# Row sums of a hybrid layer's FFN as one task that requests ahead, and a compression bank that isn't cleared

## The chip, the cores and the metric

The kernel runs on one core of one Trainium2 chip. The metric is the device time of one execution in microseconds (us). The core's engines run their own queues of instructions and wait for each other through semaphores: TensorE (PE in the profile: matrix products), VectorE (DVE), ScalarE (ACT), GpSimd (POOL) and SyncE (SP, which only issues DMAs here; POOL issues some too).

## The reference

One decoder layer for 256 tokens of width 2048, in float32. One input projection feeds two groups of heads, gated linear attention (GLA) and a sparse attention (NSA); an output projection joins them, and a SwiGLU feed-forward network (FFN) follows. The part of NSA that the change touches is the compression of keys and values: 15 overlapping blocks of 32 tokens for each of 2 heads get a position vector added and go through a small network.

```python
def hybrid_layer(...):
    n = rms_norm(x, attn_norm_g)
    proj = n @ w_in
    ...
    h = x + jnp.concatenate([gla_out, nsa_out], axis=-1) @ w_out
    m = rms_norm(h, ffn_norm_g)
    return h + (jax.nn.silu(m @ w_gate) * (m @ w_up)) @ w_down

def compress(u, pos, w1, w2):
    blocks = u[:, :, cmp_idx] + pos
    flat = blocks.reshape(b_, hk, n_cmp, CMP_BLOCK * dh)
    return jax.nn.silu(flat @ w1) @ w2
```

## The kernel before

**Products.** Each float32 product is made of three matmuls: an operand is split into a high part (`hi`, rounded by ACT, L144) and a low part (`lo`, what is left, by DVE, L145), and `chunk` (L292) issues hi x hi, hi x lo and lo x hi. Weights of the two projections come in blocks of 1 MB (`raw`, three buffers) through SP's queue; a block is asked for when the third block before it has been split. These products run from the start of the kernel almost without a break to about 420 us; the FFN fills the rest.

**The FFN's row sums.** Most of the FFN runs as a scheme that needs 7 products of sub-blocks in place of 8 (L1164), at the price of sums of rows of the weights. Sixteen of these sums (a column block f and a pair of row blocks: (0,4), (1,2) to (1,5), (2,7) to (9,7), (10,2), (10,5), (10,7)) are made long ahead, beside the projections and mixers: `sum_rows` asks for two tiles of rows through SP (0.5 MB each, `gate` and `up`, L1091), makes four additions on DVE in place (L1096) and stores the two results to DRAM through POOL's queue (L1100). The FFN fetches them from there (L1153).

**What sets the order.** The order on each engine is that of the program. `drive` takes the projections' matmuls one group of three at a time, 2 units each. Whenever a count of units reaches `rate[0]`, the first task of `background` goes one step; and for each `pace` units a step of `urgent` or `later` goes (the mixers' small work). So `rate` says how many units lie between two steps of a sum: 12, then 26, 18, 14 and 14 in the five stages. A sum takes nine steps: the request, two empty ones, four additions, the store, one empty.

**The mixers' places.** Scores are normalised with a power of -0.5 on POOL (`rsqrt_`, L220): DVE L631 in front and L633 behind it in GLA's output, where L637 and L638 then scale (L655 makes a low part); L731, L732 in front and L734, L737 behind it for NSA's keys, which PE then transposes (L217).

**Compression.** `w1_rows` (L771) asks through POOL's queue for a half of a layer's weights, as two tiles; `positions` (L780) adds the position vectors on DVE, two instructions; then 16 matmuls (L796) add up into four groups of 30 rows of a PSUM bank, at a distance of 32. The bank is cleared first by DVE (L788) as the groups' last two rows are never written but are read with the rest (L803). Two such groups of 16 belong to the key, two to the value. A group's matmul j needs tile j // 8 of the weights.

**Buffers.** Rows of the sums, weights of the compression and other tiles of 4 KB per partition share one pool of 24 (`g4`): each takes the place of an older tile, and waits for all that read it.

Of the kernel before, what the change touches and what calls it, by code (L numbers as in the profile page):

```python
# [8 lines left out]
F32 = mybir.dt.float32  # L9
# [3 lines left out]
ALU = mybir.AluOpType  # L13
AX = mybir.AxisListType

P = 128
# [10 lines left out]
NCMP = 15  # L27
# [10 lines left out]
def kernel(  # L38
# [736 lines left out]
    def positions(w, half, new):  # L775

        blk, j0 = new([16, 2, NCMP]), 16 * half
        for h in range(2):
            u = st["uT"][:, w, h, j0:j0 + 240].rearrange("p (n j) -> p j n", j=16)
            TT(blk[:, :, h, :], u, pos[:, w, j0:j0 + 16].unsqueeze(2).to_broadcast([P, 16, NCMP]), ALU.add)  # L780
        return blk

    def compress():

        nxt = [st["rows"], w1_rows(1)]
        for w in range(2):
            ph = bank()
            nc.vector.memset(ph[:, :P], 0.0)  # L788
            for half in range(2):
# [4 lines left out]
                for j in range(16):  # L794
                    g = 32 * (j % 4)
                    mm(ph[g:g + N2, :P], blk[:, j].rearrange("p h n -> p (h n)"), r[j // 8][:, j % 8, :], start=(half == 0 and j < 4),  # L796
                       stop=(half == 1 and j >= 12), tile_position=(0, g), skip_group_check=True)
                    if j % 16 == 15:
                        yield
# [285 lines left out]
    def sum_rows(f, pair):  # L1085

        n_tiles[0] += 1
        gate, up = g4([2, 512]), g4([2, 512])
        for to, m in ((gate, w_gate), (up, w_up)):
            with behind(last["dma"]):  # L1090
                nc.sync.dma_start(to, m[0][2 * pair * P:(2 * pair + 2) * P, f * FB:(f + 1) * FB].rearrange("(k p) w -> p k w", p=P))  # L1091
        for _ in range(3):
            yield True
        for o, i in ((up[:, 0], up[:, 1]), (up[:, 1], gate[:, 1]), (gate[:, 1], up[:, 0]), (gate[:, 0], gate[:, 1])):
            with behind(last["d"]):
                TT(o, o, i, ALU.add)  # L1096
            yield True
        to = row_sums[f, pair] = [dp.tile([P, 2, 512], F32, name=f"sums{i}_{f}_{pair}") for i in range(2)]
        for part, a in zip(to, (up, gate)):
            nc.gpsimd.dma_start(part, a)  # L1100
        for _ in range(1):
            yield True
# [265 lines left out]
    background += [sum_rows(f, pair) for f in sorted(SUMS) for pair in SUMS[f]]  # L1368
    rate[0] = 12
# [3 lines left out]
    rate[0] = 26  # L1373
# [3 lines left out]
    rate[0] = 18  # L1377
    drive([proj(C_NQ + 512, ev_nq(1))], 2.5)
    rate[0] = 14
# [3 lines left out]
    rate[0] = 14  # L1383
# [43 lines left out]
```

## Time and profile before

| | |
|---|---|
| median of 3 executions | 1103.51 us (1102.64 to 1104.92) |
| profiled execution | 1103.67 us |
| its span | 1102.0 us |
| FFN's matmuls, L1164 and L292 on `ftwo` | 431.7 us and 221.1 us busy |
| DVE L1096, 64 additions | 0.69 us each |
| DMA from 50 to 100 us | 350 GB/s |

The span is what the trace covers; the rest of the execution's time lies around it. A timeline row reads: start, duration, engine, line, operation, output and inputs, partitions x elements; in brackets, how long the engine sat idle before it and for which engine's result. PE is TensorE's matmuls. Waits are also listed by group: engine and line that waited, what it waited for, the sum in us, how often, the longest. A chain's shares tell whose work the end of the kernel hangs on.

### The profile page before, as it was taken

The page shows a single profiled execution, that of the slowest core. Times are in us where ns is not written, and L with a number is a line of the kernel's source. Part 1 is how long each engine was busy: PE and PEld are TensorE (multiplying, and loading weights), DVE is VectorE, ACT ScalarE, POOL GpSimd, SP SyncE. Part 2 cuts the span into 40 slices and gives each one's busy share as a digit, 9 for nine tenths or more (in the row PEclk, how much of TensorE's full clock was granted, in tenths as well). Part 3 has the DMA queues.
Part 4 walks back from the last instruction along what each step waited for, and adds up shares of the span by engine and source line. Part 5 has one row for each costly group of instructions (what it writes and reads, how often), then busy time and mean ns, then how long its engine had stood idle before and what let it go on. Part 6 is the DMA issues. An engine that isn't in the chain of part 4 may idle for free.

```text
span 1102.0 us, 14594 instructions
## 1 busy us (share of the span) xinstructions
PE 1094.4 (99%) x5290; PEld 900.6 (82%) x5290; DVE 991.5 (90%) x1277; ACT 742.0 (67%) x1009; POOL 73.1 (7%) x134
## 2 busy tenths in 40 slices
PE   9999999999999999999999999999999999999998
PEld 8888888987787877888888888888888888888886
DVE  6678879987799688997999999999999999999997
ACT  6645557555675587667586866768586866768685
POOL 4110001132100000000000000000000000000000
PEclk9999999999999999999999999999999999999999
DMA  7999988467864547785566657576566657576773
GB/s 269 340 340 368 354 295 292 160 226 285 287 229 173 191 153 244 234 318 188 182 230 210 214 200 251 175 257 210 202 230 210 215 199 251 174 259 231 234 230 114
DMA packets 124850, 259.61 MB, mean 236 GB/s; under 512 B 6709, under 2 KB 8793, under 8 KB 124778
## 3 DMA queue, kind: packets, MB, share of 16 engines
q1 hardware_dynamic: 113514, 219.86, 58.3%
q0 software_dynamic: 10368, 37.75, 9.3%
q10 hardware_dynamic: 896, 1.07, 0.3%
q8 instruction: 41, 0.67, 0.2%
q14 instruction: 31, 0.25, 0.1%
HBM read 239.78 MB, written 18.87 MB: 235 GB/s over the span
## 4 chain that ended last, share of the span: by engine, by line
PE 94%; DVE 3%; DMA 1%; POOL 1%; ACT 1%; issue 1%; ACTq 0%; SPq 0%; DVEq 0%; POOLq 0%
PE bank L292 47%; PE bank L1164 39%; PE bank L217 3%; PE bank L1305 2%; PE bank L889 1%; PE bank L962 1%; POOL sm L220 1%; DMA raw<-in_w_in_dram 1%; DMA g<-in_w_up_dram 1%; DVE lo L145 0%; PE bank L597 0%; DVE g L637 0%; PE bank L796 0%; DVE g L592 0%; DVE g L638 0%
## 5 line engine op out<-in xcount | busy, mean ns | idle before, releaser
L1164 PE MATMUL bank<-ftwo,g 128*128 128x512 f32 x1848 | 431.7, 392 | 0.2 <-ACT ftwo L654 0.2
L1164 PEld LDWEIGHTS bank<-ftwo,g 128*128 128x128 f32 x1848 | 342.5, 188 | 76.5 <-DVE ftwo L655 3.3
L292 PE MATMUL bank<-hi,g 128*128 128x512 f32 (+1 forms) x1088 | 325.2, 377 | 0.5 <-ACT hi L332 0.5
L655 DVE TENSOR_TENSOR ftwo<-fraw,ftwo 128x1536 fp32r<-128x1536 f32 (+1 forms) x130 | 257.6, 1982 | 8.2 <-ACT ftwo L654 6.8
L654 ACT ACTIVATE ftwo<-fraw 128x1536 fp32r<-128x1536 f32 (+1 forms) x130 | 217.0, 1671 | 32.0 <-DMA fraw<-in_w_up_dram 22.9
L292 PE MATMUL bank<-ftwo,g 128*128 128x512 f32 x960 | 221.1, 391 | 0.0
L292 PEld LDWEIGHTS bank<-hi,g 128*128 128x128 f32 x1088 | 192.0, 188 | 31.1 <-issue 1.4
L292 PEld LDWEIGHTS bank<-ftwo,g 128*128 128x128 f32 x960 | 179.2, 188 | 39.2 <-ACT bank L1276 1.9
L292 PE MATMUL bank<-lo,g 128*128 128x512 f32 (+3 forms) x544 | 193.9, 376 | 0.4 <-DVE lo L333 0.3
L144 ACT ACTIVATE hi<-raw 128x1024 fp32r<-128x1024 f32 (+3 forms) x124 | 130.5, 1057 | 86.0 <-PE bank L292 64.1
L145 DVE TENSOR_TENSOR lo<-raw,hi 128x1024 fp32r<-128x1024 f32 (+3 forms) x124 | 149.7, 1217 | 35.3 <-ACT hi L144 34.8
L654 ACT ACTIVATE ftwo<-g 128x1024 fp32r<-128x1024 f32 x74 | 78.2, 1057 | 69.9 <-DVE g L1195 40.6
L292 PEld LDWEIGHTS bank<-lo,g 128*128 128x128 f32 x544 | 98.5, 189 | 15.0 <-DVE lo L333 0.8
L655 DVE TENSOR_TENSOR ftwo<-g,ftwo 128x1024 fp32r<-128x1024 f32 x74 | 90.2, 1218 | 10.5 <-ACT ftwo L654 10.5
L655 DVE TENSOR_TENSOR ftwo<-fsum,ftwo 128x1024 fp32r<-128x1024 f32 x74 | 90.1, 1217 | 0.0
L654 ACT ACTIVATE ftwo<-fsum 128x1024 fp32r<-128x1024 f32 x74 | 77.5, 1048 | 6.9 <-DVE fsum L1197 5.7
L1288 ACT COPY g<-bank 128x512 f32<-128x512 f32 x80 | 45.9, 589 | 38.8 <-PE bank L292 37.1
L1195 DVE TENSOR_TENSOR g<-fraw 128x1024 f32<-128x1024 f32 x56 | 67.4, 1216 | 0.0
L1276 ACT COPY bank<-g 128x512 f32<-128x512 f32 x80 | 45.2, 593 | 14.4 <-DVE f L1225 13.2
L654 ACT ACTIVATE g<-bank 128x512 fp32r<-128x512 f32 x46 | 27.2, 598 | 32.1 <-PE bank L217 26.6
L217 PE MATMUL bank<-ident,g 128*128 128x128 f32 (+3 forms) x230 | 43.3, 276 | 0.2 <-DVE g L737 0.2
L1153 POOL DMA_DIRECT2D g<-sums x16 | 8.5, 533 | 510.8 <-DVE ftwo L655 482.2
(244 smaller groups left out, 899.8 us busy)
## 6 DMA issues: line engine op xcount, KB each, us to landing
fraw<-in_w_gate_dram SPq DMA_DIRECT2D x86, 512.0 KB, 4.0
fraw<-in_w_down_dram SPq DMA_DIRECT2D x42, 1024.0 KB, 5.1
raw<-in_w_in_dram SPq DMA_DIRECT2D x36, 1024.0 KB, 7.6
fraw<-in_w_up_dram SPq DMA_DIRECT2D x70, 512.0 KB, 4.8
sums<-g POOLq DMA_DIRECT2D x32, 512.0 KB, 6.4
raw<-in_w_out_dram SPq DMA_DIRECT2D x16, 1024.0 KB, 5.2
g<-in_w_gate_dram SPq DMA_DIRECT2D x16, 512.0 KB, 7.3
g<-in_w_up_dram SPq DMA_DIRECT2D x16, 512.0 KB, 8.9
```

Source lines behind the costliest of these rows:

```text
L144: act(h[:, i:i + n], r[:, k + i:k + i + n], AF.Copy)
L145: last["d"] = TT(o[:, i:i + n], r[:, k + i:k + i + n], f32(h[:, i:i + n]), ALU.subtract)
L217: return nc.tensor.transpose(o, i, ident[:n, :n])
L220: nc.gpsimd.tensor_tensor(o, i, mhalf[:i.shape[0], :i.shape[1]], ALU.pow)
L292: last["mm"] = mm(bk[t], a[:, k, t * P:(t + 1) * P], m[:, off:off + w], start=(first_ and k == 0 and i == 0), stop=(end and k == 3 and i = ...
L654: act(hi, ps, AF.Copy)
L655: last["d"] = TT(lo, ps, f32(hi), ALU.subtract)
L1164: mm(banks[q], x, m, start=todo[q] == total[q], stop=todo[q] == 1)
L1195: TT(s1, r[:, 1:3], r[:, 3:4].to_broadcast([P, 2, 512]), ALU.add)
L1276: nc.scalar.copy(banks[qs[n][t]], h_sb[n][:, t, :])
L1288: nc.scalar.copy(h_sb[n][:, t, :], bs[t])
L1305: mm(bk, u, m, start=(first and i == 0), stop=(end and i == 2), skip_group_check=onto)
```

## The change

Two things change.

The sixteen tasks become one, `all_sums`. It asks for the first sum's rows, passes three steps, and then for each sum first asks for the next sum's rows, has one empty step, makes four additions in four steps, and stores along with the last step. A sum has five steps instead of nine, and the rates are 22, 46, 32, 24 (and 24 to the end) instead of 12, 26, 18, 14, 14, which gives 110 units for a sum in the first stage in place of 108.

In the compression, DVE no longer clears the bank. `positions` makes a tile of 32 columns for each j, whose last two POOL sets to zero (four new MEMSETs), and the matmuls write all 32 rows of a group.

```diff
@@ -774,18 +774,19 @@
 
     def positions(w, half, new):
 
-        blk, j0 = new([16, 2, NCMP]), 16 * half
+        full, j0 = new([16, 32]), 16 * half
+        nc.gpsimd.memset(full[:, :, N2:], 0.0)
+        blk = full[:, :, :N2].rearrange("p j (h n) -> p j h n", h=2)
         for h in range(2):
             u = st["uT"][:, w, h, j0:j0 + 240].rearrange("p (n j) -> p j n", j=16)
             TT(blk[:, :, h, :], u, pos[:, w, j0:j0 + 16].unsqueeze(2).to_broadcast([P, 16, NCMP]), ALU.add)
-        return blk
+        return full
 
     def compress():
 
         nxt = [st["rows"], w1_rows(1)]
         for w in range(2):
             ph = bank()
-            nc.vector.memset(ph[:, :P], 0.0)
             for half in range(2):
                 r = nxt.pop(0)
                 blk = positions(w, half, g2) if w or half else st["blk"]
@@ -793,7 +794,7 @@
                     yield
                 for j in range(16):
                     g = 32 * (j % 4)
-                    mm(ph[g:g + N2, :P], blk[:, j].rearrange("p h n -> p (h n)"), r[j // 8][:, j % 8, :], start=(half == 0 and j < 4),
+                    mm(ph[g:g + 32, :P], blk[:, j], r[j // 8][:, j % 8, :], start=(half == 0 and j < 4),
                        stop=(half == 1 and j >= 12), tile_position=(0, g), skip_group_check=True)
                     if j % 16 == 15:
                         yield
@@ -1082,24 +1083,31 @@
     SUMS[0] = (4,)
     row_sums = {}
 
-    def sum_rows(f, pair):
-
-        n_tiles[0] += 1
-        gate, up = g4([2, 512]), g4([2, 512])
-        for to, m in ((gate, w_gate), (up, w_up)):
+    def rows_for(f, pair):
+
+        res = g4([2, 512]), g4([2, 512])
+        for to, m in zip(res, (w_gate, w_up)):
             with behind(last["dma"]):
                 nc.sync.dma_start(to, m[0][2 * pair * P:(2 * pair + 2) * P, f * FB:(f + 1) * FB].rearrange("(k p) w -> p k w", p=P))
+        return res
+
+    def all_sums(todo):
+
+        nxt = rows_for(*todo[0])
         for _ in range(3):
             yield True
-        for o, i in ((up[:, 0], up[:, 1]), (up[:, 1], gate[:, 1]), (gate[:, 1], up[:, 0]), (gate[:, 0], gate[:, 1])):
-            with behind(last["d"]):
-                TT(o, o, i, ALU.add)
+        for at, (f, pair) in enumerate(todo):
+            gate, up = nxt
+            if at + 1 < len(todo):
+                nxt = rows_for(*todo[at + 1])
             yield True
-        to = row_sums[f, pair] = [dp.tile([P, 2, 512], F32, name=f"sums{i}_{f}_{pair}") for i in range(2)]
-        for part, a in zip(to, (up, gate)):
-            nc.gpsimd.dma_start(part, a)
-        for _ in range(1):
-            yield True
+            for o, i in ((up[:, 0], up[:, 1]), (up[:, 1], gate[:, 1]), (gate[:, 1], up[:, 0]), (gate[:, 0], gate[:, 1])):
+                with behind(last["d"]):
+                    TT(o, o, i, ALU.add)
+                yield True
+            to = row_sums[f, pair] = [dp.tile([P, 2, 512], F32, name=f"sums{i}_{f}_{pair}") for i in range(2)]
+            for part, a in zip(to, (up, gate)):
+                nc.gpsimd.dma_start(part, a)
 
 
     rf = kp.tile([P, NT], F32, name="rf")
@@ -1365,22 +1373,21 @@
 
     drive([proj(C_LR, ev_go(0), ((0, 256), (256, 272)), first_chunk)], 2)
     constants()
-    background += [sum_rows(f, pair) for f in sorted(SUMS) for pair in SUMS[f]]
-    rate[0] = 12
+    background.append(all_sums([(f, pair) for f in sorted(SUMS) for pair in SUMS[f]]))
+    rate[0] = 22
     drive([proj(C_GO + 512, ev_go(1)), proj(0, ev_conv(0, to_qk(qq, kk))), proj(512, ev_conv(4, to_qk(kk, qq))),
            proj(1024, ev_conv(8, to_v(0))), proj(1536, ev_conv(12, to_v(1)))], 1.5)
     later.append(gla_mix())
-    rate[0] = 26
+    rate[0] = 46
     drive([proj(C_KC, ev_kc), proj(C_KS, ev_kv(0)),
            proj(C_KW, ev_kv(1), ((0, 256), (256, 280))), proj(C_NQ, ev_nq(0))], 2.5)
     later.append(nsa_mix())
-    rate[0] = 18
+    rate[0] = 32
     drive([proj(C_NQ + 512, ev_nq(1))], 2.5)
-    rate[0] = 14
+    rate[0] = 24
     drive([w_out_half(0)], 2.4)
     drain(urgent)
     drain(later)
-    rate[0] = 14
     drive([w_out_half(1)], 6)
 
     for f in range(NFB):
```

Lines behind 774 move: L780 becomes L782, L796 L797, L1096 L1106, L1100 L1110, L1153 L1161; L1091 keeps its number. Numbers in tiles' names differ between the two kernels; in an order's row "x2" stands for two like instructions.

The first place is the key's second group of the compression. DVE's queue in front of it, before (`sm` are the mixers' small sums, `g_437` is the tile of `positions` that the second group reads, `lo` a split of a projection's weights):

```order
L631 TENSOR_SCALAR sm_2451<-sm_2446 128x2
L145 TENSOR_TENSOR lo_2617<-raw_2614,hi_2616 128x2x512
L633 TENSOR_SCALAR sm_2451<-sm_2451 128x2
L631 TENSOR_SCALAR sm_2480<-sm_2475 128x2
L655 TENSOR_TENSOR g_416_2493<-bank_2494,g_415_2492 128x512
```

Further down, up to the second group's `positions`:

```order
L637 SCALAR_TENSOR_TENSOR g_428_2534<-bank_2507,sm_2530,gng 128x256 x2
L638 TENSOR_TENSOR g_428_2534<-g_428_2534,g_15_127 128x256 x2
L749 SCALAR_TENSOR_TENSOR g_319_1977<-bank_2556,kgain,g_318_1976 128x2x128
L749 SCALAR_TENSOR_TENSOR g_319_1977<-bank_2562,kgain,g_318_1976 128x2x128
L655 TENSOR_TENSOR g_416_2493<-bank_2569,g_415_2492 128x512
L1096 TENSOR_TENSOR g_361_2231<-g_361_2231 128x512
L780 TENSOR_TENSOR g_437_2603<-g_283_1777,cols 128x16x15 x2
L145 TENSOR_TENSOR lo_2692<-raw_2685,hi_2691 128x2x512
```

The same after:

```order
L631 TENSOR_SCALAR sm_2446<-sm_2441 128x2
L145 TENSOR_TENSOR lo_2610<-raw_2607,hi_2609 128x2x512
L631 TENSOR_SCALAR sm_2475<-sm_2470 128x2
L633 TENSOR_SCALAR sm_2446<-sm_2446 128x2
L633 TENSOR_SCALAR sm_2475<-sm_2475 128x2
L637 SCALAR_TENSOR_TENSOR g_396_2450<-bank_2372,sm_2446,gng 128x256 x2
L638 TENSOR_TENSOR g_396_2450<-g_396_2450,g_14_126 128x256 x2
L637 SCALAR_TENSOR_TENSOR g_402_2479<-bank_2462,sm_2475,gng 128x256 x2
L638 TENSOR_TENSOR g_402_2479<-g_402_2479,g_15_127 128x256 x2
L655 TENSOR_TENSOR g_404_2488<-bank_2489,g_403_2487 128x512
L631 TENSOR_SCALAR sm_2524<-sm_2519 128x2
L145 TENSOR_TENSOR lo_2614<-raw_2607,hi_2613 128x2x512
```

and up to `positions`:

```order
L637 SCALAR_TENSOR_TENSOR g_416_2528<-bank_2501,sm_2524,gng 128x256 x2
L638 TENSOR_TENSOR g_416_2528<-g_416_2528,g_15_127 128x256 x2
L749 SCALAR_TENSOR_TENSOR g_308_1971<-bank_2549,kgain,g_307_1970 128x2x128
L749 SCALAR_TENSOR_TENSOR g_308_1971<-bank_2555,kgain,g_307_1970 128x2x128
L655 TENSOR_TENSOR g_404_2488<-bank_2562,g_403_2487 128x512
L782 TENSOR_TENSOR g_425_2595<-g_275_1773,cols 128x16x15 x2
L782 TENSOR_TENSOR g_476_2817<-g_275_1773,cols 128x16x15
L145 TENSOR_TENSOR lo_2689<-raw_2682,hi_2688 128x2x512
```

The addition ahead of `positions` has left, the two L631 and L633 stand next to each other with both L637 pairs behind them, and the L788 between them is gone.

POOL's queue there, before (L220 is a power, `sums` a store of a sum, L771 the requests for the weights: `g_429` and `g_430` are the two tiles of the key's second half):

```order
L220 TENSOR_TENSOR sm_2416<-sm_2416,mhalf 128x2
L220 TENSOR_TENSOR sm_2451<-sm_2451,mhalf 128x2
L771 DMA g_429_2539<-in_cmp_k_w_dram 128x8x128
L220 TENSOR_TENSOR sm_2480<-sm_2480,mhalf 128x2
L771 DMA g_430_2541<-in_cmp_k_w_dram 128x8x128
L771 DMA g_435_2599<-in_cmp_v_w_dram 128x8x128
L220 TENSOR_TENSOR sm_2530<-sm_2530,mhalf 128x2
L771 DMA g_436_2601<-in_cmp_v_w_dram 128x8x128
```

and after, where these two are `g_417` and `g_418`:

```order
L220 TENSOR_TENSOR sm_2411<-sm_2411,mhalf 128x2
L1110 DMA sums_7_7_2625<-g_268_1742 128x1024
L220 TENSOR_TENSOR sm_2446<-sm_2446,mhalf 128x2
L220 TENSOR_TENSOR sm_2475<-sm_2475,mhalf 128x2
L771 DMA g_417_2533<-in_cmp_k_w_dram 128x8x128
L220 TENSOR_TENSOR sm_2524<-sm_2524,mhalf 128x2
L771 DMA g_418_2535<-in_cmp_k_w_dram 128x8x128
L771 DMA g_423_2591<-in_cmp_v_w_dram 128x8x128
L771 DMA g_424_2593<-in_cmp_v_w_dram 128x8x128
L778 MEMSET g_425_2595 128x16x2
L778 MEMSET g_476_2817 128x16x2
```

The second tile stood ahead of the power of `sm_2530` and stands behind it now (there `sm_2524`); the store of a sum has come ahead of the power of `sm_2446`; the MEMSET of `positions`' tile follows the values' first two requests.

The second place is on DVE ahead of the first keys' normalisation, before:

```order
L592 COPY_PREDICATED g_312_1927<-lmask,bank_1962 128x128
L1096 TENSOR_TENSOR g_291_1820<-g_291_1820 128x512
L592 COPY_PREDICATED g_311_1926<-lmask,g_312_1927 128x128 x2
L731 TENSOR_SCALAR sm_1987<-sm_1982,rx_123 128x2
L145 TENSOR_TENSOR lo_2091<-raw_2088,hi_2090 128x2x536
L732 TENSOR_SCALAR sm_1987<-sm_1987 128x2
L145 TENSOR_TENSOR lo_2095<-raw_2088,hi_2094 128x2x536
L734 TENSOR_SCALAR sm_1987<-sm_1987,rx 128x2
L564 TENSOR_TENSOR g_81_567<-g_81_567,g_80_566 128x32x8
```

and after:

```order
L592 COPY_PREDICATED g_301_1922<-lmask,bank_1957 128x128
L731 TENSOR_SCALAR sm_1981<-sm_1976,rx_123 128x2
L592 COPY_PREDICATED g_300_1921<-lmask,g_301_1922 128x128 x2
L732 TENSOR_SCALAR sm_1981<-sm_1981 128x2
L145 TENSOR_TENSOR lo_2084<-raw_2081,hi_2083 128x2x536
L734 TENSOR_SCALAR sm_1981<-sm_1981,rx 128x2
L145 TENSOR_TENSOR lo_2088<-raw_2081,hi_2087 128x2x536
L737 TENSOR_SCALAR g_315_1986<-bank_1706,sm_1981 128x128 x2
```

The addition between the copies is gone; L732 stands ahead of both splits and L734 between them, where they stood one split later.

The third place is SP's queue behind the constants, where rows of the sums and blocks of the projection's weights are asked for, before:

```order
L135 DMA raw_690<-in_w_in_dram 128x4x512
L1091 DMA g_78_562<-in_w_gate_dram 128x2x512
L1091 DMA g_79_563<-in_w_up_dram 128x2x512
L135 DMA raw_732<-in_w_in_dram 128x4x512
L135 DMA raw_774<-in_w_in_dram 128x4x512
L1091 DMA g_96_669<-in_w_gate_dram 128x2x512
L1091 DMA g_97_670<-in_w_up_dram 128x2x512
L135 DMA raw_811<-in_w_in_dram 128x4x512
L135 DMA raw_854<-in_w_in_dram 128x4x512
L1091 DMA g_111_759<-in_w_gate_dram 128x2x512
L1091 DMA g_112_760<-in_w_up_dram 128x2x512
L1091 DMA g_124_845<-in_w_gate_dram 128x2x512
```

and after (the block that is raw_690 before is raw_685 after, raw_732 keeps its name, raw_774 is raw_768):

```order
L135 DMA raw_685<-in_w_in_dram 128x4x512
L1091 DMA g_77_562<-in_w_gate_dram 128x2x512
L1091 DMA g_78_563<-in_w_up_dram 128x2x512
L1091 DMA g_87_618<-in_w_gate_dram 128x2x512
L1091 DMA g_88_619<-in_w_up_dram 128x2x512
L135 DMA raw_732<-in_w_in_dram 128x4x512
L1091 DMA g_101_717<-in_w_gate_dram 128x2x512
L1091 DMA g_102_718<-in_w_up_dram 128x2x512
L135 DMA raw_768<-in_w_in_dram 128x4x512
L135 DMA raw_812<-in_w_in_dram 128x4x512
L135 DMA raw_848<-in_w_in_dram 128x4x512
L1091 DMA g_115_808<-in_w_gate_dram 128x2x512
```

Ahead of raw_732 stand two sets of rows instead of one, and the next set stands ahead of raw_768.

## The prediction

> **What bounds the kernel now.** I read the page's head, then TensorE's waits, and only then the place in the trace where the change moves something.
>
> ```profile
> span 1102.0 us, 14594 instructions
> PE 1094.4 (99%) x5290; PEld 900.6 (82%) x5290; DVE 991.5 (90%) x1277; ACT 742.0 (67%) x1009; POOL 73.1 (7%) x134
> PE 94%; DVE 3%; DMA 1%; POOL 1%; ACT 1%; issue 1%; ACTq 0%; SPq 0%; DVEq 0%; POOLq 0%
> ```
>
> TensorE (PE) is busy for 1094.4 of 1102.0 us, and 94% of the chain that ended last is its work. VectorE (DVE) is busy 90% of the time, but a late DVE instruction costs only when PE comes to stand behind it. All such stands, for the whole kernel (engine, line, what it waited for: us, times, longest):
>
> ```profile
> PE bank L207 <- DVE g L201: 1.3, 1, 1.3
> PE bank L796 <- DVE g L780: 1.1, 1, 1.1
> PE bank L292 <- ACT hi L332: 0.5, 1, 0.5
> PE bank L292 <- DVE lo L333: 0.3, 1, 0.3
> PE bank L1164 <- ACT ftwo L654: 0.2, 1, 0.2
> PE bank L217 <- DVE g L737: 0.2, 1, 0.2
> ```
>
> L207, L332 and L333 are the first steps of the kernel, and L1164 is the FFN; the change touches neither. Two rows are left: 1.1 us where the compression's second group of matmuls waits for `positions`, and 0.2 us where a pair of key transposes waits for L737. Around them (start, duration, engine, line; the idle time before it in brackets):
>
> ```profile
> 253.52 1.08 PE L796 MATMUL bank<-g,g 128*30 128x128 f32 x32 [1.10 <-DVE g L780]
> ...
> 210.72 0.50 PE L217 MATMUL bank<-ident,g 128*128 128x128 f32 x2 [0.16 <-DVE g L737]
> ```
>
> PE was through with what it had at 253.52 - 1.10 = 252.42. What the change can win, if both vanish, is 1.10 + 0.16 = **1.26 us**, plus at most a few tenths of restart around them. That is under 0.2% of the span (2.2 us), about what a measurement of this kernel can tell from no change.
>
> **The requests in front of the additions.** DVE's largest wait that concerns the change is this one:
>
> ```profile
> DVE g L1096 <- DMA g<-in_w_up_dram: 11.6, 5, 5.1
> 69.41 0.69 DVE L1096 TENSOR_TENSOR g<-g 128x512 f32<-128x512 f32 x1 [5.08 <-DMA g<-in_w_up_dram]
> 70.75 1.22 DVE L145 TENSOR_TENSOR lo<-raw,hi 128x1024 fp32r<-128x1024 f32 x1
> 72.92 0.39 PE L292 MATMUL bank<-lo,g 128*128 128x512 f32 x1
> ```
>
> With the rows asked for a whole sum ahead (five ticks of 22 units instead of three ticks of 12) these 11.6 us should go. But even after the longest of them, 5.08 us, the split at 70.75 ended at 71.97 and PE first read it at 72.92, 0.95 us later. No row of PE's list names these lines. So **11.6 us of DVE idleness are worth 0**; the cover is the work that PE has in hand, and it is 0.95 us at its thinnest. Were the cover gone, PE would stand for the excess over 0.95 us; the change thickens it here.
>
> The number of additions (16 sums of four), loads and stores stays; only places change. An addition counts where it stands just before something that PE waits for.
>
> **The key transposes (210 us).** DVE rows of before:
>
> ```profile
> 202.95 0.69 DVE L1096 TENSOR_TENSOR g<-g 128x512 f32<-128x512 f32 x1
> 210.23 0.61 DVE L737 TENSOR_SCALAR g<-bank,sm 128x128 f32<-128x128 f32 x2
> ```
>
> In the changed order the addition at 202.95, among the L592 copies, stands elsewhere and none takes its place (the second order shown with the change). From there to L737 each step hands on to the next, so L737 comes up to its pitch of 0.60 earlier, and the wait of 0.16 goes: **-0.16** (0 if something that PE releases holds the chain in between). Late next is nothing here: the changed order puts its next addition behind the two splits that follow.
>
> **The compression's second group (253 us).** This is the term that decides.
>
> ```profile
> 241.92 0.17 DVE L633 TENSOR_SCALAR sm<-sm 128x2 f32<-128x2 f32 x1 [0.58 <-POOL sm L220]
> 242.07 0.68 DVE L655 TENSOR_TENSOR g<-bank,g 128x512 fp32r<-128x512 f32 x1
> 242.67 0.86 DVE L637 SCALAR_TENSOR_TENSOR g<-bank,sm,gng 128x256 f32<-128x256 f32 x2
> 243.45 0.75 DVE L638 TENSOR_TENSOR g<-g,g 128x256 f32<-128x256 f32 x2
> ...
> 244.42 0.17 DVE L788 MEMSET bank<- 128x128 f32 x1
> 244.50 0.81 DVE L637 SCALAR_TENSOR_TENSOR g<-bank,sm,gng 128x256 f32<-128x256 f32 x2
> 245.22 0.75 DVE L638 TENSOR_TENSOR g<-g,g 128x256 f32<-128x256 f32 x2
> 245.89 0.16 DVE L631 TENSOR_SCALAR sm<-sm 128x2 f32<-128x2 f32 x1
> ...
> 251.85 0.68 DVE L1096 TENSOR_TENSOR g<-g 128x512 f32<-128x512 f32 x1
> 252.45 1.01 DVE L780 TENSOR_TENSOR g<-g,cols 128x240 f32<-128x240 f32 x2
> ```
>
> Pitches count, since each starts before the one ahead has ended. The addition at 251.85 stands directly in front of `positions` at 252.45: its pitch is 0.60. In the changed order it is gone from there (-0.60), and the memset's pitch of 0.08 with it. Against that the changed order asks for two powers one behind the other, and the L637 work of both stands behind the second. In before the first power returned at 241.92; the second, 0.72 us long (row below), returns at about 242.65, and until then DVE has only small instructions. Then come an L633, 0.1, two pairs of L637 and L638 and the L655, by their pitches 0.78 + 0.67 (as in the second pair) + 0.72 + 0.67 + 0.60 = 3.44: L631 starts at 242.65 + 0.1 + 3.44 = 246.2 instead of 245.89, so +0.3, the memset's going counted in. From there the chain is as before as far as the addition. So L780 starts at 252.45 + 0.3 - 0.60 = 252.15 and ends at 253.16 instead of 253.46: the group starts **0.30 us earlier**, and the wait of 1.10 is 0.80. The ends are +0.6 (the second power 1.62 long instead of 0.72) and -1.10 (no wait left).
>
> But the group needs a second thing, the weights' rows, and here POOL's queue is rearranged:
>
> ```profile
> 240.29 1.59 POOL L220 TENSOR_TENSOR sm<-sm,mhalf 128x2 f32<-128x2 f32 x1 [2.99 <-DVE sm L631]
> 241.84 0.95 POOL L771 DMA_DIRECT2D g<-in_cmp_k_w_dram  x1
> 242.81 0.72 POOL L220 TENSOR_TENSOR sm<-sm,mhalf 128x2 f32<-128x2 f32 x1
> 243.49 0.94 POOL L771 DMA_DIRECT2D g<-in_cmp_k_w_dram  x1
> 246.14 1.62 POOL L220 TENSOR_TENSOR sm<-sm,mhalf 128x2 f32<-128x2 f32 x1 [0.83 <-DVE sm L631]
> ...
> DMA to landing us min/median/max: 4.7/5.7/7.6
> ```
>
> Of the key's two tiles the second was issued at 243.49, ahead of the power at 246.14. In the changed order it stands behind that power, so it is issued at about 246.14 + 1.62 + 0.2 = 248.0 and lands, by the six issues of L771 in this stretch, 4.7 to 7.6 us later: 252.7 to 255.6, at the median 253.7. PE wants it halfway through the group: 1.08 / 2 = 0.54 us after the group's start, now 253.52 - 0.30 = 253.22, that is at 253.76. **The two meet**: at the median the wait is 0, at the slowest 1.9 us; before, the tile had some 5 us to spare. I take the median, the middle of the only six rows there are, and add 0.1 for the lopsided spread. That tile also takes a buffer that a store of the sums must have left; the store follows the addition that takes the place of the one at 239.29, so it is issued at about 240.0 and lands by L1100's row at 242.9 to 248.7:
>
> ```profile
> 239.29 0.69 DVE L1096 TENSOR_TENSOR g<-g,g 128x512 f32<-128x512 f32 x1
> ...
> DMA to landing us min/median/max: 2.9/6.4/8.7
> ```
>
> Only the slowest would hold the issue back, by 0.7 us.
>
> The power itself shows why it is slow: 0.72 us alone, 1.62 with the split of 1.22 us (L145) beside it; it ends 0.6 us after that split does. [...]
>
> **The four memsets and 32 columns.** POOL's memsets of the last two columns have 128x16x2 elements; the nearest row is
>
> ```profile
> 255.16 0.33 POOL L814 MEMSET g<- 128x256 f32 x1
> ```
>
> so each is between 0 and 0.33 us. The one that the second group needs stands behind three L771 issues of about 0.94 us, from 248.0 on: 248.0 + 2.8 + 0.33 = 251.1, before L780's 252.15. If that cover of 1 us went, L780 would be later by the excess. The rows for the values, queued in the same row, are for the next two groups, which stand far behind in PE's order. The matmul's moving side stays 128 columns wide, so 32 instead of 30 columns of weights is 0, between -0.05 and +0.05 us in all over 128 matmuls that take 34 ns each (1.08 / 32). The values' memset of a bank is worth 0: no row shows PE waiting there.
>
> **Rows asked for earlier, and the raw loads.** In the crowded stretch the SP queue now carries two sets of rows ahead of a block of the projection's weights (raw) where it carried one, some blocks before today's place with two (the third order shown with the change). The stretch, and today's place:
>
> ```profile
> 50.00:100.00 50.00, 50.00 (x226) 41.38 (x225) 37.03 (x49) 27.65 (x33) 3.20 (x6) 1.00 0.95 350
> ...
> 74.96 2.01 ACT L144 ACTIVATE hi<-raw 128x1024 fp32r<-128x1024 f32 x2 [3.72 <-DMA raw<-in_w_in_dram]
> 76.82 2.35 DVE L145 TENSOR_TENSOR lo<-raw,hi 128x1024 fp32r<-128x1024 f32 x2
> 81.08 0.39 PE L292 MATMUL bank<-lo,g 128*128 128x512 f32 x1
> ```
>
> At 350 GB/s (last column; the share of the DMA engines ahead of it is 0.95) one more set of 1.05 MB is 3.0 us. The other three rows are the block that today is asked for behind two sets of rows: ACT waits 3.72 us for it, its first split is done at 76.82 + 1.22 = 78.04, and PE reads that at 81.08, 3.0 us later. So a block behind two sets just passes, and 0 is taken; were the cover the 0.95 us of above, it would be 3.0 - 0.95 = 2.05. After the change the pair of sets stands ahead of an earlier block, and this one has a single set ahead.
>
> **Sum**, against the profiled execution (span 1102.0, its own time 1103.67, 1.67 us lying around the span): -0.16 - 0.30 + 0.1 = -0.36: 1103.3. The median of the three runs is 0.16 below that execution; I set the forecast to it: 1103.51 - 0.36 = 1103.15, so **1103.1 us**, no change that can be measured.
>
> **The rivals.**
> - *Both waits vanish.* If the second power doesn't hold DVE and the tile lands at 4.7 us: -1.26 and the restart, at most -1.6: 1101.9. For it: the addition directly ahead of L780 really leaves. Against it: 0.60 is less than 1.10. Chance 0.13.
> - *The wait changes its owner.* The second group stands for the key's second tile, because its issue is behind the power. It decides from a landing after 254.06 (253.52 + 0.54), which is 6.1 us after issue; half of the six took 5.7 us or more, the longest 7.6. Price: 255.6 - 254.06 = 1.5, with the slowest store 2.2, less 0.16: up to +2.0, so 1104.0 at the middle and 1105.5 at the end. Slower than before. Chance 0.24.
> - *Raw weights come late* behind two sets of rows between 45 and 75 us, and PE stands for L144/L145. It decides from a delay beyond the cover of 0.95 us; up to 2.05 a block, 4.1 over two: 1105.2 to 1107.2. Against it: no such wait on PE today although a block took its place behind two sets already. Chance 0.07.
> - *The change does not do what it says*: the rows are asked for early, but their buffers come free late (two sets are live now), and DVE waits as today; PE's waits stay: 0, so 1103.5. Chance 0.10.
>
> The forecast has the rest, 0.46.
>
> **How the numbers follow.** The range takes in the forecast, both ends of its terms and the first two rivals but for their tails: 1101.7 to 1105.4. Faster by over 0.2% needs 2.2 us, more than the two waits hold, so only the spread of the measurement gives it: 0.06. Slower by over 0.2%: the third rival and the slowest part of the second, 0.07 + 0.06 = 0.13. The rest, 0.81, is within 0.2%.
>
> **What would show it.** Right: the list of PE's waits has no L737, L796 (then L797) still waits for the L782 of `positions`, 0.4 to 1.0 us; no L1106 on DVE waits for a DMA of a microsecond or more. The second rival shows as L797 waiting for a DMA from in_cmp_k_w within the group; the third as L292 waiting for ACT or DVE between 45 and 75 us. The forecast is wrong if PE has a new wait anywhere in the first 420 us that isn't in the list above, or if the FFN, whose order is the same, changes its length.

## The result, and the profile after

The changed kernel takes **1111.11 us** (median of six, 1110.26 to 1112.48) against 1102.75 us (1102.52 to 1104.92) for the kernel before: a ratio of 1.0071, with a 95% interval of 1.0060 to 1.0081. It is slower by 0.7%, and the time lies 5.7 us above the upper end of the range. The profiled execution of the changed kernel took 1111.26 us.

The head of its page and the shares of the chain that ended last:

```profile
span 1109.6 us, 14589 instructions
PE 1096.5 (99%) x5290; PEld 901.7 (81%) x5290; DVE 991.6 (89%) x1275; ACT 741.5 (67%) x1009; POOL 72.8 (7%) x138
PE 90%; DVE 4%; DMA 2%; issue 1%; ACT 1%; POOL 1%; ACTq 0%; POOLq 0%; DVEq 0%
```

The work is the same, and the span is 7.6 us longer. PE's share of the chain that ended last fell from 94% to 90%, and DMA, which had 1%, has 2%. So PE stands more often, and some of it goes back to transfers. TensorE's waits (engine, line, what it waited for: us, times, longest):

```profile
PE bank L597 <- ACT g L610: 3.0, 1, 3.0
PE bank L217 <- DVE g L737: 1.3, 1, 1.3
PE bank L207 <- DVE g L201: 1.3, 1, 1.3
PE bank L292 <- ACT hi L332: 0.9, 1, 0.9
PE bank L797 <- DMA g<-in_cmp_k_w_dram: 0.7, 1, 0.7
PE bank L597 <- DVE g L592: 0.6, 1, 0.6
PE bank L797 <- issue: 0.5, 1, 0.5
...
PE bank L292 <- DVE lo L145: 0.3, 1, 0.3
```

The first row is new, a stand of 3.0 us in GLA's scores (L597). The wait for the key's normalisation (L737) was to vanish and grew from 0.2 to 1.3. L797, which had 1.1 us for `positions` (as L796), has 0.7 for weights and 0.5 for which the profile names no releaser (`issue`). What stands behind the first two, as the timeline shows it (start, duration, engine, line; idle time before and its releaser in brackets):

```profile
198.94 0.56 POOL L1110 DMA_DIRECT2D sums<-g  x1 [9.67 <-DVE g L592]
...
204.03 0.48 DVE L713 SCALAR_TENSOR_TENSOR g<-bank,rx,g 128x256 fp32r<-128x256 f32 x1 [2.04 <-DMA sums<-g]
...
212.05 0.50 PE L217 MATMUL bank<-ident,g 128*128 128x128 f32 x2 [1.33 <-DVE g L737]
...
223.11 0.58 POOL L1110 DMA_DIRECT2D sums<-g  x1 [12.05 <-DVE g L1106]
...
230.32 0.84 ACT L748 ACTIVATE g<-bank,kgain 128x256 fp32r<-128x256 f32 x2 [5.92 <-DMA sums<-g]
231.05 1.05 ACT L144 ACTIVATE hi<-raw 128x1024 fp32r<-128x1024 f32 x1
232.00 0.28 ACT L610 ACTIVATE g<-bank 128x128 f32<-128x128 f32 x1
...
232.32 0.71 PE L597 MATMUL bank<-g,g 128*128 128x128 f32 x4 [3.05 <-ACT g L610]
```

L713 and L748 read nothing of the sums: L713 makes the low part of the values (`vl`), L748 the high part of the keys (`kh`). What they wait for is the *store* of a sum (`sums<-g`), since their new tile takes the place of that sum's tile in the pool of 24, and the tile is free only once its store has landed. In the kernel before, no instruction of ACT or DVE waits for a store. ACT stands 5.92 us in front of L748, with a split and L610 queued behind it, and PE stands 3.05 us for L610. The chain that ended last has it as one line of descent (start, us on the chain, what):

```profile
222.12 0.70 DVE g L1106
222.82 0.29 issue
223.11 7.14 DMA sums<-g
...
230.32 0.09 ACT g L748
230.41 0.28 issue
230.69 0.47 ACT g L748
231.16 0.94 ACT hi L144
232.10 0.18 ACT g L610
...
232.32 1.36 PE bank L597 x8
```

An addition at 222.12 releases a store, the store is on its way for 7.14 us, and L748, the split, L610 and PE follow. And the stand costs more than its length. In windows of 2 us (columns: window, its length, busy time of PE, PEld, DVE, ACT and POOL, PE's granted clock, DMA share, GB/s):

```profile
228.00:230.00 2.00, 1.27 (x6) 0.77 (x5) 0.52 (x3) 0.00 (x0) 0.00 (x0) 1.00 1.02 406
230.00:232.00 2.00, 0.00 (x0) 0.00 (x0) 0.00 (x0) 1.68 (x4) 0.00 (x0) 1.00 0.99 385
232.00:234.00 2.00, 1.68 (x11) 1.68 (x12) 1.86 (x3) 1.00 (x6) 0.00 (x0) 0.79 0.10 39
234.00:236.00 2.00, 2.00 (x12) 2.00 (x11) 1.35 (x7) 0.00 (x0) 0.71 (x1) 0.50 0.03 8
236.00:238.00 2.00, 2.00 (x17) 2.00 (x17) 1.68 (x6) 0.00 (x0) 0.00 (x0) 0.86 0.00 0
```

From 232 to 238 us the granted clock is 0.79, 0.50 and 0.86: 2 x (0.21 + 0.50 + 0.14) = 1.7 us of work lost. L797's two rows add up to what it stood before, so the longer span comes out as 3.05 (L610) + 1.7 (clock) + 1.17 (L737, 1.33 less 0.16) + 0.59 (L592) + 0.3 (L145) + 0.4 (L332) = 7.2 of 7.6 us. The last of these belongs to the kernel's first steps, which the change does not touch.

One more thing was not where the front part put it. ACT's queue there, before (`g_318` is `kh`):

```order
L144 ACTIVATE hi_2271<-raw_2269 128x2x536
L748 ACTIVATE g_318_1976<-bank_2133,kgain 128x2x128
L748 ACTIVATE g_318_1976<-bank_2144,kgain 128x2x128
L558 ACTIVATE g_351_2159<-g_81_567 128x8x32
```

and after (`g_307` is `kh`):

```order
L144 ACTIVATE hi_2269<-raw_2263 128x2x536
L577 ACTIVATE g_349_2220<-g_80_567 128x256
L579 ACTIVATE g_349_2220<-g_80_567,sm_2221 128x128 x2
L144 ACTIVATE hi_2429<-raw_2427 128x2x512
L144 ACTIVATE hi_2433<-raw_2427 128x2x512
L748 ACTIVATE g_307_1970<-bank_2134,kgain 128x2x128
L748 ACTIVATE g_307_1970<-bank_2141,kgain 128x2x128
L144 ACTIVATE hi_2508<-raw_2506 128x2x512
L610 ACTIVATE g_352_2230<-bank_2279 128x128
```

The pair of L748 moved from behind the block of `raw_2269` to behind two later splits, close ahead of L610, though the code that issues it is untouched. So, unlike what the front part says, the order on each engine is only roughly that of the program; by what rule an instruction moves is not known. In the runs below where the keys' high part has a buffer of its own (e3, e6, e7), its pair stands ahead of L577 again, as before.

### The profile page after: what moved, and what is told of

It is laid out like the page before. It is cut to its first block, busy times and chain, and to the rows that moved or that the text cites. A ratio compares the mean times of both kernels' runs of the same rounds, so it can differ in the third digit from the quotient of the medians.

```text
span 1109.6 us, 14589 instructions
## 1 busy us (share of the span) xinstructions
PE 1096.5 (99%) x5290; PEld 901.7 (81%) x5290; DVE 991.6 (89%) x1275; ACT 741.5 (67%) x1009; POOL 72.8 (7%) x138
## 4 chain that ended last, share of the span: by engine, by line
PE 90%; DVE 4%; DMA 2%; issue 1%; ACT 1%; POOL 1%; ACTq 0%; POOLq 0%; DVEq 0%
PE bank L292 44%; PE bank L1172 39%; PE bank L217 3%; PE bank L1313 2%; DMA sums<-g 1%; DVE lo L145 1%; PE bank L890 1%; PE bank L963 1%; DMA raw<-in_w_in_dram 1%; DMA g<-in_cmp_k_w_dram 1%; POOL sm L220 1%; ACT hi L144 0%; PE bank L597 0%; DVE g L1106 0%; DVE g L592 0%
## 5 line engine op out<-in xcount | busy, mean ns | idle before, releaser
L292 PE MATMUL bank<-hi,g 128*128 128x512 f32 (+1 forms) x1088 | 325.0, 377 | 0.9 <-ACT hi L332 0.9
L292 PE MATMUL bank<-ftwo,g 128*128 128x512 f32 x960 | 221.2, 391 | 0.0
L292 PEld LDWEIGHTS bank<-hi,g 128*128 128x128 f32 x1088 | 192.7, 189 | 31.1 <-ACT hi L332 1.6
L292 PEld LDWEIGHTS bank<-ftwo,g 128*128 128x128 f32 x960 | 179.2, 188 | 39.3 <-ACT bank L1284 1.9
L292 PE MATMUL bank<-lo,g 128*128 128x512 f32 (+3 forms) x544 | 194.3, 377 | 0.6 <-DVE lo L333 0.3
L145 DVE TENSOR_TENSOR lo<-raw,hi 128x1024 fp32r<-128x1024 f32 (+3 forms) x124 | 150.2, 1218 | 47.5 <-ACT hi L144 46.9
L292 PEld LDWEIGHTS bank<-lo,g 128*128 128x128 f32 x544 | 99.0, 190 | 15.2 <-DVE lo L333 0.8
L217 PEld LDWEIGHTS bank<-ident,g 128*128 128x128 f32 (+3 forms) x230 | 31.0, 141 | 14.0 <-issue 2.0
```

The lines of the kernel that those rows point to most:

```text
L145: last["d"] = TT(o[:, i:i + n], r[:, k + i:k + i + n], f32(h[:, i:i + n]), ALU.subtract)
L217: return nc.tensor.transpose(o, i, ident[:n, :n])
L292: last["mm"] = mm(bk[t], a[:, k, t * P:(t + 1) * P], m[:, off:off + w], start=(first_ and k == 0 and i == 0), stop=(end and k == 3 and i = ...
```

## The experiments

The theory, from the rows above: **mixers' tiles take buffers of sums whose stores are still on their way** (the buffer theory). Its rivals: the compression's edits cost the time; or the requests as such do, two sets of rows being live and on the DMA queues at once (the crowding theory). Each run below is timed against the kernel before on the same chip; medians of before were 1103.28 to 1103.94 us.

**The two parts apart.** `e1` is the changed kernel with the compression as before; `e2` is the kernel before with only the compression's edits.

> Only the sums' part of the change; the compression is as before (bank cleared on DVE, 30 columns). Buffer theory (the key's tile takes the buffer of a sum whose store is still on its way): the wait of ACT L748 for a store's landing stays at about 6 us and the time is that of the changed kernel, 1110 to 1112. Rival, the compression's four memsets and requests on POOL cost it: 1103 to 1105.

> Only the compression's part on the kernel before. Buffer theory: no wait of ACT L748 for a store; within 0.7 us of before, 1102.2 to 1103.5; PE's wait for positions may shrink by 0.1 as the DVE memset's pitch of 0.08 goes. Rival, the compression's part costs it: 1108 or more.

Measured: e1 1110.45 us, ratio 1.0069 (1.0046 to 1.0091); e2 1103.69 us, 0.9998 (0.9989 to 1.0008). The sums carry the whole loss; the compression's edits cost nothing and bring nothing, though e2 lies 0.2 us above the range expected for it and PE's stand at L797, which might have shrunk from 1.10 us, is 1.49. In e1's profile, taken from the slowest of its four executions (1114.48 us), L748 stands 6.7 us for a store, and PE 3.8 us for L610.

**Buffers of their own for the keys.** The keys' two tiles no longer take a place in the pool of 24. Four buffers of another pool, `g2`, pay for it.

```diff
-    g4, g2, g1, small = slot(gp, "g4", 24, LINE), slot(s2p, "g2", 13), ...
+    g4, g2, g1, small = slot(gp, "g4", 24, LINE), slot(s2p, "g2", 9), ...
+    own = slot(s2p, "own", 2, LINE)
...
-                    st[name] = g4(shape, F32R)
+                    st[name] = (own if name[0] == "k" else g4)(shape, F32R)
```

> The changed kernel, but the selected keys' two tiles (kh, kl) have buffers of their own, outside the pool of 24 (another pool is cut from 13 to 9 tiles for the room). The additions, requests and stores stay in their places. Buffer theory: the 5.7 us lost between 224 and 236 us go, with PE's wait for L610 (3.0), the wait for L592 may stay (0.6), the granted clock there is 1.00 instead of 0.79; the wait of L713 for a store (2.0 on DVE, 1.3 on PE) stays, as the value's and window tiles still take such buffers: 1104.5 to 1106.5. Rival, the places of the additions on DVE cost it: 1110 to 1112.

Measured: 1106.51 us, 1.0030 (1.0019 to 1.0041); of a loss of 8.4 us 3.2 are left. No L748 (L750 here) waits for a store, and the stand of L597 is gone; but the pair also stands earlier in ACT's order, at 215.17, and the run doesn't tell the buffer from the place. What is left is the other store (L715 here is L713 of the changed kernel, L294 its L292):

```profile
204.25 0.48 DVE L715 SCALAR_TENSOR_TENSOR g<-bank,rx,g 128x256 fp32r<-128x256 f32 x1 [3.85 <-DMA sums<-g]
...
212.87 0.81 PE L294 MATMUL bank<-lo,g 128*128 128x256 f32 x2 [1.86 <-DVE lo L147]
```

DVE stands 3.85 us for it, is late with the split that PE needs, and PE stands 1.86 us. The windows that follow:

```profile
212.00:214.00 2.00, 1.13 (x5) 1.13 (x6) 2.00 (x5) 0.96 (x3) 0.00 (x0) 0.71 0.08 6
214.00:216.00 2.00, 2.00 (x11) 2.00 (x11) 2.00 (x6) 2.00 (x5) 0.00 (x0) 0.50 0.92 254
216.00:218.00 2.00, 2.00 (x17) 2.00 (x17) 2.00 (x5) 1.14 (x3) 0.00 (x0) 0.94 0.69 267
```

The granted clock falls to 0.50 again, 1.7 us, in this profiled execution (1107.47 us); of the seven that were timed, five kept a mean clock of 0.999 or 1.000. A further 0.7 us, `L1174 <- DVE ftwo L657` in the FFN, is a wait that the changed kernel doesn't have.

**Only the high part's buffer.** As e3, but for `kh` alone (`g2` then keeps 11 tiles).

```diff
-                    st[name] = g4(shape, F32R)
+                    st[name] = (own if name == "kh" else g4)(shape, F32R)
```

> The changed kernel with a buffer of its own for the first of the selected keys' two tiles (kh) only. The other one (kl, written by DVE L749) then takes the very buffer that kh had, behind the same store. Buffer theory: the wait moves from ACT L748 to DVE L749 (which stands as L751 in this kernel), about 5 us, and PE waits for DVE's splits or copies instead: 1108 to 1111. Rival, that the loss comes from ACT's queue alone: 1105 to 1106.5, as with both tiles on their own.

Measured: 1111.68 us, 1.0069 (1.0049 to 1.0089), no gain, and 0.7 us above the range expected. The wait went over to the low part, `kl` (L751 is L749 of the changed kernel):

```profile
229.96 0.88 DVE L751 SCALAR_TENSOR_TENSOR g<-bank,kgain,own 128x256 fp32r<-128x256 f32 x2 [3.35 <-DMA sums<-g]
...
230.59 1.19 PE L622 MATMUL bank<-g,g 128*128 128x256 f32 x2 [3.20 <-DVE g L751]
```

With one tile fewer in the pool's turn, the next tile meets the same store (issued at 222.43 here), and PE stands 3.20 us behind it instead of 3.05. It isn't the operation that matters but whose turn it is.

**The request behind the additions.** One task as in the change, but the next rows are asked for behind this sum's stores, so that only one set is live.

```diff
             gate, up = nxt
-            if at + 1 < len(todo):
-                nxt = rows_for(*todo[at + 1])
             yield True
...
                 nc.gpsimd.dma_start(part, a)
+            if at + 1 < len(todo):
+                nxt = rows_for(*todo[at + 1])
```

> The changed kernel with the next sum's rows asked for behind this one's additions and stores instead of in front of them; five steps per sum and the rates stay, so the additions stay at about their places. One set of rows lives at a time. Buffer theory: the selected keys' tiles no longer meet a store under way, L713 neither: no DMA sums wait on ACT or DVE in 190 to 240 us, 1102.5 to 1104; DVE waits for rows again by a few us, at no cost. Rival, the additions' later places cost it: 1109 or more. Rival, both sets of rows crowd the DMA engines: also 1102.5 to 1104, but then e3 stays slow.

Measured: 1108.72 us, 1.0048 (1.0033 to 1.0063). The expectation missed. From 190 to 256 us no mixers' tile stands for a store, as expected; but at 137 us something new does:

```profile
126.18 0.49 SPq L1091 DMA_DIRECT2D g<-in_w_up_dram  x1
...
137.65 0.69 DVE L1104 TENSOR_TENSOR g<-g 128x512 f32<-128x512 f32 x1 [5.67 <-DMA g<-in_w_up_dram]
138.26 1.51 DVE L501 SCALAR_TENSOR_TENSOR g<-bank,cols,g 128x255 f32<-128x255 f32 x3
...
143.84 1.10 PE L217 MATMUL bank<-ident,g 128*128 128x128 f32 x4 [5.12 <-ACT g L520]
```

The rows were asked for at 126.18, and the addition waits for them until 137.65, with the convolution (L501) queued behind it. Its result goes through ACT's L520 to PE, which stands 5.12 us. The clock then falls to 0.50 here too (from 143.89 us). So a wait for rows, which cost nothing anywhere in the kernel before, does cost here: asking early is worth something, and this place is where.

**The phase moved.** If the turn of the buffers decides, moving all sums by a step must move the collisions. The change has three empty steps behind the first request; here there are two, one and four.

```diff
-        for _ in range(3):
+        for _ in range(2):
```

> The changed kernel with two empty steps instead of three before the first sum, so that all sums come 22 units earlier. By the order the window keys' value tile (L713) now follows no store closely, while the selected keys' tile (L748) still takes the buffer of the store that follows DVE's second addition of the sum in progress. Buffer theory: L713's wait on a store and PE's 1.3 us for L737 go, L748's wait stays or is somewhat shorter: 1107 to 1110, 1.5 to 3 us under the changed kernel. Rival, places of the additions: no change of over 0.5 us.

> The changed kernel with one empty step instead of three before the first sum: all sums 44 units earlier. By the order the store of sum (7,7)'s second half now stands just two DVE instructions ahead of the window keys' value tile (L713), which takes its buffer. Buffer theory: L713 stands for nearly a whole landing (5 to 7 us), PE behind it, with a drop of the granted clock: 1106 to 1111, though two steps less than the change is more of what mended it. Rival, that the sums only have to come early enough: 1102.5 to 1104, as with one step less.

> The changed kernel with four empty steps instead of three: all sums 22 units later. By the order the selected keys' tile takes another buffer, and L713 follows the store that it waits for by ten DVE instructions (fifteen in the changed kernel). Buffer theory: no wait of L748 for a store, L713's wait grows from 2.0 to 3 to 5 us with PE behind it: 1105 to 1108. Rival, the sums only have to come early enough: 1111 or more.

| empty steps | time, us | ratio (95%) | largest waits of PE that are new |
|---|---|---|---|
| 1 (e9) | 1112.37 | 1.0080 (1.0066 to 1.0093) | L737 3.7 and 1.0, L592 1.8 |
| 2 (e5) | 1103.40 | 0.9994 (0.9985 to 1.0004) | none over 0.6 |
| 3 (the change) | 1111.11 | 1.0071 (1.0060 to 1.0081) | L610 3.0, L737 1.3 |
| 4 (e10) | 1103.21 | 0.9995 (0.9986 to 1.0004) | none over 0.6 |

e9 came as expected in kind: L713 stands for a store and PE behind it, for 4.50 us where 5 to 7 were expected, and the time is above the 1106 to 1111 us expected. e5 and e10 missed their expectations: each was to keep or make a loss, and neither did. The order of instructions showed which tile follows which store closely, and that was taken for a price. In e10 the last store issued ahead of L713, at 206.47, has landed after 3.5 us, just before L713 starts at 209.96 without an idle time on DVE. In e5 the store ahead of L748 is issued 9 us earlier than in the changed kernel:

```profile
214.14 0.59 POOL L1110 DMA_DIRECT2D sums<-g  x1 [6.39 <-DVE g L1106]
...
220.59 0.84 ACT L748 ACTIVATE g<-bank,kgain 128x256 fp32r<-128x256 f32 x2 [3.17 <-DVE g L592]
...
224.68 0.28 ACT L610 ACTIVATE g<-bank 128x128 f32<-128x128 f32 x1 [2.30 <-DVE g L592]
```

L748 runs at 220.59 instead of 230.32. The profile puts its idle time of 3.17 us to a result of DVE that L748 doesn't read; the store lands 6.4 us after its issue, at 220.5, and in e11 below the same row is put to the store. So ACT most likely waits for the store here too, and what has gone is the price: L610, which PE needs, waits for DVE until 224.68 anyway, and no wait of PE goes back to L748. In e9 a store of the sums is issued ahead of the values' low part:

```profile
216.68 0.53 POOL L1110 DMA_DIRECT2D sums<-g  x1 [9.21 <-DVE g L1106]
...
222.97 0.88 DVE L713 SCALAR_TENSOR_TENSOR g<-bank,rx,g 128x256 fp32r<-128x256 f32 x2 [4.50 <-DMA sums<-g]
...
226.82 0.33 PE L217 MATMUL bank<-ident,g 128*128 128x128 f32 x1 [3.66 <-DVE g L737]
```

L713 stands 4.50 us and PE, through L737, 3.66. The same requests, additions, stores and live sets thus cost 9, 0, 8 and 0 us as the phase moves by a step of 22 units at a time. Crowding as such doesn't give that: the work in flight is the same in all four, and the stores take about as long in the fast ones (median of 32 stores from issue to landing: 6.7, 6.7, 6.8 and 6.6 us for 1 to 4 empty steps, 6.4 in the kernel before).

**Both remedies, and the remedy's own price.** e7 has the keys' own buffers and two empty steps; e8 has the own buffers in the kernel before.

> The changed kernel with both remedies: own buffers for the selected keys' two tiles, and one empty step less at the start. By the order no tile that the mixers write from 180 to 250 us follows a store closely. Buffer theory: no wait for a store on ACT or DVE in this stretch, the granted clock 1.00 throughout, 1101.5 to 1103.7, as before or up to 1 us less. Rival, two live sets of rows or the additions' places cost something by themselves: 1105 or more.

> The kernel before with own buffers for the selected keys' two tiles and the other pool cut from 13 to 9 tiles: what the remedy itself costs or brings. Buffer theory: nothing there waits for a store before, so 1102.5 to 1104.5. If the cut of the other pool costs time, more than that, and the runs with own tiles are to be read with that much taken off.

Measured: e7 1103.32 us, 0.9992 (0.9983 to 1.0002), with no wait of ACT or DVE for a store. e8 1107.00 us, 1.0025 (1.0015 to 1.0034), which missed: the kernel before has no store to wait for there, and the buffers were to cost little. In e8:

```profile
PE bank L1166 <- DVE ftwo L657: 2.1, 2, 1.2
PE bank L219 <- ACT g L522: 1.9, 1, 1.9
```

Both rows are new. The second ends on the path of e4's stand (L522 is L520 there), and DVE's waits for rows have grown from 11.6 us in all to 17.6. With two tiles out of the pool of 24 everything behind them takes another turn, and `g2` has 9 buffers instead of 13; which of the two makes these waits was not tried. Nor is the price of 3.1 us to be taken off e3: e7 has the same buffers and doesn't pay it. So in e3 L748's wait goes with its buffer, but e3's time is not a clean measure of that wait.

**The best version.** e5 with the compression's weights asked for through SP's queue, away from the powers on POOL.

```diff
-            nc.gpsimd.dma_start(to, (k_w1, v_w1)[i // 2]...
+            nc.sync.dma_start(to, (k_w1, v_w1)[i // 2]...
```

> The kernel with one empty step less, and the compression's weights asked for through SP's queue instead of POOL's, so that they no longer stand behind POOL's powers. If the key's second tile is late because of POOL's queue, PE's 0.6 to 0.8 us on L797 go and the time is 0.3 to 0.8 us under that of one step less, 1102 to 1103.2. If SP's queue holds loads of the projection's weights behind them, a wait of ACT L144 for raw shows: 1103.5 or more.

Measured: 1102.56 us, 0.9990 (0.9981 to 0.9999). PE's waits at L797 (0.6 and 0.2 in e5) are gone. ACT's splits wait 9.1 us for raw weights, where it was 3.6 in e5, and no wait of PE goes back to that. The store holds L748, without a price:

```profile
220.59 0.84 ACT L748 ACTIVATE g<-bank,kgain 128x256 fp32r<-128x256 f32 x2 [3.49 <-DMA sums<-g]
```

ACT stands 3.49 us for the store, and no wait of PE goes back to it. It is the one version of eleven whose interval lies below 1, and only just. The interval overlaps with that of e5, so a gain over e5 is not shown.

## Why the prediction was wrong

- **The step that failed** stands in the two sentences "The number of additions (16 sums of four), loads and stores stays; only places change. An addition counts where it stands just before something that PE waits for." A place counts in a second way: it sets when the store behind the addition is issued, and so when two buffers of the pool of 24 come free. The prediction weighed that once only, for the key's second weight tile ("Only the slowest would hold the issue back, by 0.7 us"). It didn't ask which other tiles take buffers of sums. In the changed kernel they are `vl` (2.04 us of DVE) and `kh` (5.92 us of ACT), at a price of 1.17 and, with the clock, 4.8 us on PE. Two more tiles wait for a store and cost PE nothing: one of the key's first weights (L771, 5.5 us of POOL at 172.91) and one of L873 (2.9 us of ACT). The tile for which the 0.7 us was reckoned is issued right behind its power, with no wait for a store.
- The rival "their buffers come free late (two sets are live now)" named the right resource, but with DVE's additions as those who wait, and priced it at 0. In the trace it isn't the rows that wait for buffers but the mixers' tiles.
- **L737, -0.16.** The addition did leave its place, and in e5 that wait is gone. In the changed kernel L713 stands 2.04 us for a store ahead of it, and the term became +1.17.
- **The second group, -0.30 and +0.1.** The order came as read, and the rival "The wait changes its owner" came with it:

```profile
253.24 1.61 POOL L220 TENSOR_TENSOR sm<-sm,mhalf 128x2 f32<-128x2 f32 x1 [2.78 <-DVE sm L631]
254.82 0.94 POOL L771 DMA_DIRECT2D g<-in_cmp_k_w_dram  x1
...
260.07 0.65 PE L797 MATMUL bank<-g,g 128*32 128x128 f32 x16 [0.45 <-issue]
261.38 0.64 PE L797 MATMUL bank<-g,g 128*32 128x128 f32 x16 [0.66 <-DMA g<-in_cmp_k_w_dram]
```

  The power takes 1.61 us (1.62 predicted), the tile is asked for behind it, and lands 6.5 us later, where 5.7 was taken. PE stands 0.66 us for it. The 0.45 ahead of the group has no releaser in the profile; in e1, which has the same order, the like stand of 0.44 us is put to `positions` (L780). Together that is 1.11 us where it was 1.10, so the rival's price, up to +2.0, was 0 net; in e1 it was 0.44 + 1.55 = 1.99 against 1.10. The new place comes with the sums: in e2 the second tile is issued at 242.64, ahead of the power at 246.18, as in the kernel before.
- **The rows' 11.6 us worth 0.** Of these waits one of 0.4 us is left (L1106), and nothing was won by it: right. But e4 shows that the cover of 0.95 us, "at its thinnest", held for the places of the kernel before only; at 137 us a wait of 5.67 us cost PE 5.12.
- **Raw weights late.** PE has no such wait: the rival did not come.
- **What the prediction named as its refutation** came: "a new wait anywhere in the first 420 us", L597 for L610. The loss of clock behind it (1.7 us) stood in no term.

What stays open: L713's wait was moved by the phase (e5, e10) but never taken away by a buffer of its own; by what rule L748 moved in ACT's order, and so whether e3 helped by the buffer or by the earlier place; and the loss is shown for this phase of the sums, while the two neighbouring phases have none.

## What to carry to other kernels

When a change moves a store, look up which tiles take the stored buffer next, over the whole pool and not only over the code that is edited, and put the store's landing, here 2.9 to 8.9 us with a median of 6.8, between the two. Then ask when PE needs what stands behind the waiting instruction: a wait of 3.49 us cost nothing in e11, one of 5.92 us cost PE 3.05 in the changed kernel. If a loss comes and goes as the phase of a background task is moved by one step, as here, look for a meeting of particular instructions rather than for too much work in flight. Another phase is the cheap remedy, but it holds only until an edit moves the phase again. ACT spread its wait to all that was queued behind it, so the row that PE names (L610) can be innocent.

## What the hardware showed that was not expected

The granted clock fell to 0.50 behind stands of PE of 1.86 us (e3) and 3.05 us (the changed kernel), each time at a price of 1.7 us; but in e9's profile, behind a stand of 3.66 us, it stayed at 1.00. So a stand's length alone doesn't decide it. The traces' clock records show what goes with it. Ahead of the kernel's end, each stretch at half clock lasts 3.41 to 3.42 us (233.14 to 236.56 in the changed kernel), and it begins a whole number of steps of 3.413 us after the clock first rose to 1.00 (67 steps in the changed kernel, where it rose at 4.45 us; in e9 it rose at 6.61). The table cuts the spans by these steps. Its first six windows are all those, in the traces of all thirteen kernels, that a drop followed; the last three are those with the least work of PE that none followed.

| run | window, us | PE busy in it, us | granted clock behind it |
|---|---|---|---|
| e1 | 229.48 to 232.89 | 0.04 | 0.50 |
| e4 | 140.48 to 143.89 | 0.05 | 0.50 |
| e6 | 226.74 to 230.15 | 0.65 | 0.50 |
| the change | 229.73 to 233.14 | 0.82 | 0.50 |
| e3 | 209.41 to 212.82 | 1.34 | 0.50 |
| e1 | 260.20 to 263.61 | 1.43 | 0.50 |
| e9 | 221.64 to 225.06 | 1.52 | 1.00 |
| e4 | 137.07 to 140.48 | 1.64 | 1.00 |
| e9 | 225.06 to 228.47 | 1.65 | 1.00 |

In these traces the clock halved behind each window with up to 1.43 us of work and behind none with 1.52 or more. e9's stand was cut in two by the edge of a window, with 1.52 and 1.65 us of work in the two windows. The first rise lies at another time in each trace, from 4.1 to 7.4 us (5.60 in the kernel before), so the same stand may well cost 1.7 us in one execution and nothing in the next: of the changed kernel's six, five have a mean clock of 0.998 and one has 1.000; of e9's four, the three that were not profiled have 0.997 or 0.998.

A store of 512 KB was on its way for 5.00 us (issued at 198.94) and 7.14 us (223.11) on the chain, the second while the DMA engines were wholly busy (1.02 at 406 GB/s from 228 to 230 us). Over the changed kernel's 32 stores it is 2.9 to 8.9 us.
